# Inner feed-forward blocks: the two parts of x side by side in one 512-column product

## The chip, the cores and the metric

The kernel runs on one core of a Trainium2 chip. The metric is the device time of one execution in microseconds; 989.68 is the median of three runs (989.38 to 989.70). One further execution was profiled; the rows below come from it.

## The reference, cut to what matters

A transformer layer on 512 tokens of width 1024, all in float32: a feed-forward, a mixer (two kinds of attention), a second feed-forward, and a last normalization.

```python
def rmsnorm(x, g):
    y = x * lax.rsqrt(jnp.mean(x * x, axis=-1, keepdims=True) + NORM_EPS)
    return y * g

def swiglu(x, w_in, w_out):
    gate, up = jnp.split(x @ w_in, 2, axis=-1)     # w_in: 1024 x 5632
    return (jax.nn.silu(gate) * up) @ w_out        # w_out: 2816 x 1024

h = h + 0.5 * swiglu(rmsnorm(h, ffn1_norm), ffn1_w_in, ffn1_w_out)
h = h + hybrid_mixer(rmsnorm(h, mix_norm), ...)
h = h + 0.5 * swiglu(rmsnorm(h, ffn2_norm), ffn2_w_in, ffn2_w_out)
return rmsnorm(h, final_norm)
```

The change touches the products `x @ w_in` of both feed-forwards and what follows them up to `silu(gate) * up`.

## The kernel before, in words

**Parts.** A float32 operand is kept as two `float32r` tiles: the high part is a cast by ScalarE (`A.copy`), the low part is the rest, by a VectorE subtraction. A product of two such operands takes three matmuls: high weights by high x, high weights by low x, low weights by high x (lines 217 to 219 with 512 columns of x, lines 352 to 354 with 256). Tokens are the columns of x and of every result; features are the 128 partitions. The scale of the normalization, one number per token, is multiplied in later: `bc` holds it for all partitions.

**Feed-forward.** `ffn` treats the 2816 hidden features as FB = 22 blocks of 128. The first three blocks (`plain`) are computed directly with `mm3_steps`. The other 19 are the inner blocks. For each of them the 2x2 product (gate and up by first and second half of the tokens, with the sum over the 1024 features in two halves) is written with seven products of half the size instead of eight (the Winograd form of Strassen's method). `sums_of_x` makes the sums of x that this needs (`S` 1 to 4) once for a feed-forward, in high and low parts, a few instructions at a time beside the plain blocks. `sums_of_w` makes the sums of a block's weights (T1 to T4) and the parts of all seven weight pieces, one block ahead.

**One inner block.** `piece_of(j, p)` does product p of block j. `product` is four k steps of three matmuls each, 256 columns. Four results are built up in three places: `b1` (a bank of tag "sc"), one of two standing banks `b2` (tag "mm"), and `b3` (tag "mm"). Between products ScalarE or VectorE reads a bank and writes another: p = 1 copies b1 to b2 (line 575), p = 5 copies b3 to the tile su (582), p = 6 writes b2 + su into b3 (585), p = 7 makes the second half of `up` (594) and scales both (595, 596), p = 2 and p = 4 scale the two halves of `gate` by bc (588, 599) and take Silu (589, 600). `finish` multiplies the two (606) and `put_g` splits the result in parts (372, 374). On the two standing banks one opening matmul is issued (line 565) so that later products can add to what an engine wrote there.

**Order.** The hand-written order of products is, per block, p = 1, then p = 4 of the block before, then 5, 6, 2, 3, 7 (lines 609 to 612). After each product come one step of `finish`, one step of `side` (sums_of_w of the next block) and a share of the out-projection (`out_advance`), whose steps are 512-column triples of `mm3_steps`, each group of eight ending in an update of h on VectorE (427) and needing a split piece of w_out (404 on ScalarE, 405 on VectorE). Out-projection work comes in groups when the hidden blocks in ENDS are done, so some blocks have more of it between their products than others. From the program in this order the build lays out a fixed order for every engine, by its own estimates of durations and by program order as the priority; on the chip each engine takes its instructions in that order and waits where an operand is not ready.

**Buffers.** PSUM has tags "mm" (4 banks), "sc" (3) and "pv" (1). `tmp` tiles (10) serve su, z, gg and the raw pieces of w_out. SP issues all loads.

Of the kernel before, what the change touches and what calls it, by code (L numbers as in the profile page):

```python
# [12 lines left out]
AF = mybir.ActivationFunctionType  # L13
ALU = mybir.AluOpType
AX = mybir.AxisListType

P = 128
# [27 lines left out]
def tile_hybrid(ctx, tc, xT, f1_wi, f1_wo, wm_t, wm_n, cw1, cw2, small, wm_oa, wm_ob, wm_oc, f2_wi, f2_wo, const, out):  # L45
    nc = tc.nc
    V, A, PE = nc.vector, nc.scalar, nc.tensor
# [4 lines left out]
    def f(ap):  # L52
        return ap.bitcast(F32)

    def ps(tag="mm"):
        return psp.tile([P, 512], F32, tag=tag, name=tag, bufs=NB[tag])
# [4 lines left out]
    def ps_any():  # L61
        turn[0] += 1
        return ps(wide_ps[turn[0] % 5])

    def flat(dt=F32R):
        return sb.tile([P, 1024], dt, tag="u", name="u", bufs=NU)

    def unit(dt=F32R):
        return flat(dt).rearrange("p (a t) -> p a t", a=2)
# [4 lines left out]
    def tmp():  # L74
        return sb.tile([P, 512], F32, tag="tmp", name="tmp", bufs=NTMP)
# [156 lines left out]
    def sums_of_x(xs, gcol, XF):  # L232

        t1, t2 = slice(0, 256), slice(256, 512)
        xg = [None] * 4

        def scaled(*us):
            for u in us:
                t = xg[u] = unit(F32)
                for a in range(2):  # L240
                    k = 2 * u + a
                    gc = sm[:, gcol + k : gcol + k + 1]
                    if gcol == S_G2 and u % 2 == 0:
                        V.tensor_scalar(t[:, a, :], h[:, k, :], gc, None, op0=ALU.mult)
                    else:
                        A.activation(t[:, a, :], h[:, k, :], AF.Copy, scale=gc)

        def sums(kp, n):
            a, b = xg[kp], xg[2 + kp]
            s = flat(F32).rearrange("p (s k t) -> p s k t", s=2, k=2)  # L250
            if n == 0:
                V.tensor_tensor(s[:, 0], a[:, :, t2], b[:, :, t2], op=ALU.add)
                V.tensor_tensor(s[:, 1], s[:, 0], a[:, :, t1], op=ALU.subtract)
                s2[kp] = s[:, 1]
            else:
                V.tensor_tensor(s[:, 0], a[:, :, t1], a[:, :, t2], op=ALU.subtract)
                V.tensor_tensor(s[:, 1], b[:, :, t1], s2[kp], op=ALU.subtract)
            return s

        def high(s):  # L260
            sh = flat().rearrange("p (s k t) -> p s k t", s=2, k=2)
            A.copy(sh, s)
            return sh

        def low(s, sh, n):
            sl = flat().rearrange("p (s k t) -> p s k t", s=2, k=2)
            V.tensor_tensor(sl, s, f(sh), op=ALU.subtract)
            for m in range(2):
                XF["S", 2 * n + m + 1].extend((sh[:, m, k], sl[:, m, k]) for k in range(2))


        s2 = [None] * 2
        scaled(0)
        yield
        scaled(2)
        yield
        sa = sums(0, 0)
        yield
        scaled(1)
        sb_ = sums(0, 1)  # L280
        ha = high(sa)
        yield
        scaled(3)
        low(sa, ha, 0)
        yield
        hb = high(sb_)
        sc = sums(1, 0)
        yield
        low(sb_, hb, 1)
        sd = sums(1, 1)  # L290
        hc = high(sc)
        yield
        low(sc, hc, 0)
        hd = high(sd)
        yield
        low(sd, hd, 1)
        yield
        for name, ks, t in (("A11", 0, t1), ("A12", 4, t1), ("A22", 4, t2)):
            XF[name].extend((xs[k][:, 0, t], xs[k][:, 1, t]) for k in range(ks, ks + 4))

    def load_raw(wi, j):
        t = double()
# [43 lines left out]

    def product(o, w, x, first):

        for k in range(4):
            c = slice(k * P, (k + 1) * P)  # L350
            new = first and k == 0
            PE.matmul(o, w[0][:, c], x[k][0], start=new, stop=False, skip_group_check=not first)  # L352
            PE.matmul(o, w[0][:, c], x[k][1], start=False, stop=False, skip_group_check=not first)  # L353
            PE.matmul(o, w[1][:, c], x[k][0], start=False, stop=k == 3, skip_group_check=not first)  # L354

    def ffn(xs, acc, wi, wo, plain, gnext):

# [2 lines left out]
        bc = rcol = None  # L360
        gs, held = {}, []
        XF = {n: [] for n in ("A11", "A12", "A22", ("S", 1), ("S", 2), ("S", 3), ("S", 4))}
# [6 lines left out]
        def put_g(j, gg):  # L369
            u = unit()  # L370
            gs[j] = u
            A.copy(u[:, 0, :], gg)
            yield
            V.tensor_tensor(u[:, 1, :], gg, f(u[:, 0, :]), op=ALU.subtract)
            yield
# [130 lines left out]

        rc_at, bc_at = ((2, 6), (3, 4)) if early else ((0, 3), (1, 1))
        side.append(sums_of_x(xs, gcol, XF))
        done = []

# [13 lines left out]
        for n in range(2 * plain):  # L524
# [16 lines left out]
            else:  # L541
                wh, wl = next_w(2)
                o = ps_any()
# [16 lines left out]

        t1, t2 = slice(0, 256), slice(256, 512)

        banks = [ps()[:, t1] for _ in range(2)]
        for o in banks:
            PE.matmul(o, xs[0][:, 0, :P], xs[0][:, 0, t1], start=True, stop=True)

        live = {}
        later = []

        def piece_of(j, p):  # L570
            if p == 1:
                live[j] = ps("sc")[:, t1], banks[j % 2], None, None, None
                b1, b2 = live[j][:2]
                product(b1, WF.pop((j, "B11")), XF["A11"], True)
                A.copy(b2, b1)
                return
            b1, b2, b3, su, z = live[j]
            if p == 5:
                b3, su, z = ps()[:, t1], tmp(), tmp()
                live[j] = b1, b2, b3, su, z  # L580
                product(b3, WF.pop((j, "T1")), XF["S", 1], True)
                A.copy(su[:, t1], b3)
            elif p == 6:
                product(b2, WF.pop((j, "T2")), XF["S", 2], False)
                V.tensor_tensor(b3, b2, su[:, t1], op=ALU.add)
            elif p == 2:
                product(b1, WF.pop((j, "B21")), XF["A12"], False)
                V.tensor_tensor(z[:, t1], b1, bc[:, t1], op=ALU.mult)
                A.activation(z[:, t1], z[:, t1], AF.Silu)
            elif p == 3:  # L590
                product(b3, WF.pop((j, "B22")), XF["S", 4], False)
            elif p == 7:
                product(b2, WF.pop((j, "T3")), XF["S", 3], False)
                V.tensor_tensor(su[:, t2], b2, su[:, t1], op=ALU.add)
                V.tensor_tensor(su[:, t1], b3, bc[:, t1], op=ALU.mult)
                V.tensor_tensor(su[:, t2], su[:, t2], bc[:, t2], op=ALU.mult)
            elif p == 4:
                product(b2, WF.pop((j, "T4")), XF["A22"], False)
                V.tensor_tensor(z[:, t2], b2, bc[:, t2], op=ALU.mult)
                A.activation(z[:, t2], z[:, t2], AF.Silu)  # L600
                del live[j]
                later.append(finish(j, su, z))

        def finish(j, su, z):
            gg = tmp()
            V.tensor_tensor(gg, su, z, op=ALU.mult)
            yield from put_g(j, gg)

        order = []
        for j in range(plain, FB):  # L610
# [3 lines left out]
        for n, (j, p) in enumerate(order):  # L614
            if p == 1 and j + 1 < FB:
                side.append(sums_of_w(raws, wi, j + 1, WF))
            piece_of(j, p)
            while later and next(later[0], later) is later:
                later.pop(0)
            side_step()  # L620
            if p == 6 and j in ENDS:
                outs.append(out_steps(ENDS.index(j)))
            out_advance(0.7 if j >= ENDS[-2] else 0.6 if j < ENDS[1] else 1.0)
            if j >= FB - 1 and not side and len(opiece) < 4:
                out_split()
# [38 lines left out]
    xs = []  # L664
    first = []
# [33 lines left out]
    A.activation(late, f(xs[KB - 1][:, 0, 0:1]), AF.Copy, scale=0.0)  # L699
    state["squares"] = [(k, acc, late) for k in range(KB)]  # L700
    xs, acc = ffn(xs, acc, f1_wi, f1_wo, NP1, S_GM)


# [550 lines left out]
    for g in (1, 0):  # L1254
        for i in range(4):
            s = Swa(g, i)
            s.name, s.needs, s.share = ("s", g, i), [] if g else ["q10"], SHARE_S
            stages.append(s)
    for g in range(2):
        for i in range(4):  # L1260
            for b in (1, 2) if i else (0,):
                s = Nsa(g, i, b)
# [6 lines left out]


    ffn(nxs, nacc, f2_wi, f2_wo, NP2, None)


# [90 lines left out]
```

## Time and profile before

| | us |
|---|---|
| runs, median (lowest to highest) | 989.68 (989.38 to 989.70) |
| the profiled execution | 989.41 |
| its span | 987.5 |
| TensorE matmul busy | 972.7 (98%), 6228 matmuls |
| VectorE busy | 799.8 (81%) |
| ScalarE busy | 507.2 (51%) |
| DMA queue, all loads and stores | 92.59 MB, 27.1% of 16 engines' span |

The span is from the first to the last instruction; the execution's time is 1.9 us longer. A busy share is an average over stages: the inner blocks run from 43 to 335 us and from 661 to 950 us of the span, the mixer lies between. Matmuls overlap, so a matmul's listed duration is longer than the distance to the next one's start. VectorE and ScalarE instructions with no wait between them overlap by less than a tenth of a microsecond. The granted clock of TensorE is 1.00 (2.4 GHz) in all stretches used here.

### The profile page before, as it was taken

Reading aid. Unit: us, or ns where it says so; the run is one execution under the profiler, and the core shown is the slowest. Engines: PE = TensorE matmul, PEld = TensorE weight load, DVE = VectorE, ACT = ScalarE, POOL = GpSimd, SP = SyncE. Lnnn points to the kernel's source line nnn. Section 1 sums busy time; section 2 is a strip of 40 time slices with the busy share of each in tenths; the row PEclk is TensorE's granted clock in tenths of the full one; section 3 lists DMA queues with packets and bytes.
Section 4 is the critical chain, followed back from the end, with each engine's and each line's share of the span. In section 5 each row is a group of like instructions: output and inputs, shape, how many; then the busy total and the mean of one; then the engine's idle time right before and its main releaser. Section 6 shows DMA issues by size and latency. Waiting matters only on the chain.

```text
span 987.5 us, 15987 instructions
## 1 busy us (share of the span) xinstructions
PE 972.7 (98%) x6228; PEld 870.4 (88%) x6228; DVE 799.8 (81%) x1459; ACT 507.2 (51%) x1037; POOL 3.8 (0%) x7
## 2 busy tenths in 40 slices
PE   9999999999999999999999999999999999999997
PEld 7889999999999889888777878889999999999996
DVE  6999788787796575788799989999978878789664
ACT  8655344353444355554678776745434435344354
POOL 0000000000000000000000000000000000000000
PEclk9999999999999999999999999999999999999999
DMA  8142413233124313123310212224231322412112
GB/s 313 44 154 102 150 44 139 76 107 131 62 86 144 125 43 106 43 71 107 130 43 8 79 44 75 86 70 162 82 136 52 130 84 99 149 44 97 45 42 86
DMA packets 36075, 93.61 MB, mean 95 GB/s; under 512 B 4384, under 2 KB 8864, under 8 KB 36000
## 3 DMA queue, kind: packets, MB, share of 16 engines
q1 hardware_dynamic: 36000, 92.59, 27.1%
q8 instruction: 49, 0.80, 0.3%
q14 instruction: 26, 0.21, 0.1%
HBM read 88.87 MB, written 2.10 MB: 92 GB/s over the span
## 4 chain that ended last, share of the span: by engine, by line
PE 91%; DVE 5%; ACT 2%; issue 1%; DMA 1%; POOL 0%; SPq 0%; DVEq 0%; ACTq 0%
PE mm L353 9%; PE mm L352 9%; PE mm L354 9%; PE sc L217 8%; PE sc L219 8%; PE sc L218 8%; PE mm L217 4%; PE mm L219 4%; PE mm L218 4%; PE sc L353 3%; PE sc L354 3%; PE sc L352 3%; PE mm L936 2%; PE pv L973 2%; PE pv L974 2%; PE mm L792 1%
## 5 line engine op out<-in xcount | busy, mean ns | idle before, releaser
L354 PE MATMUL mm<-u 128*128 128x256 f32 x760 | 214.7, 283 | 0.0
L352 PE MATMUL mm<-u 128*128 128x256 f32 x760 | 214.4, 282 | 0.3 <-ACT u L328 0.3
L353 PE MATMUL mm<-u 128*128 128x256 f32 x760 | 214.6, 282 | 0.0
L352 PEld LDWEIGHTS mm<-u 128*128 128x128 f32 x760 | 144.5, 190 | 7.7 <-ACT u L328 0.5
L353 PEld LDWEIGHTS mm<-u 128*128 128x128 f32 x760 | 144.8, 191 | 5.5
L217 PE MATMUL sc<-u 128*128 128x512 f32 x364 | 144.3, 396 | 2.3 <-ACT u L404 2.1
L354 PEld LDWEIGHTS mm<-u 128*128 128x128 f32 x760 | 144.8, 191 | 0.5
L218 PE MATMUL sc<-u 128*128 128x512 f32 x364 | 143.6, 395 | 0.0
L219 PE MATMUL sc<-u 128*128 128x512 f32 x364 | 142.7, 393 | 0.0
L217 PE MATMUL mm<-u 128*128 128x512 f32 x220 | 89.8, 408 | 0.0
L219 PE MATMUL mm<-u 128*128 128x512 f32 x220 | 86.9, 395 | 0.0
L218 PE MATMUL mm<-u 128*128 128x512 f32 x220 | 86.5, 393 | 0.0
L354 PE MATMUL sc<-u 128*128 128x256 f32 x304 | 86.0, 283 | 0.3 <-DVE u L325 0.3
L353 PE MATMUL sc<-u 128*128 128x256 f32 x304 | 85.9, 283 | 0.0
L352 PE MATMUL sc<-u 128*128 128x256 f32 x304 | 85.7, 282 | 0.0
L219 PEld LDWEIGHTS sc<-u 128*128 128x128 f32 x364 | 68.4, 188 | 17.6 <-DVE u L405 1.8
L217 PEld LDWEIGHTS sc<-u 128*128 128x128 f32 x364 | 69.2, 190 | 9.7 <-ACT u L404 2.5
L404 ACT CAST u<-tmp 128x512 fp32r<-128x512 f32 (+1 forms) x96 | 55.0, 583 | 44.2 <-PE sc L219 21.0
L218 PEld LDWEIGHTS sc<-u 128*128 128x128 f32 x364 | 69.2, 190 | 6.3
L427 DVE SCALAR_TENSOR_TENSOR h<-sc,h 128x512 f32<-128x512 f32 x85 | 58.3, 686 | 11.7 <-PE sc L219 11.6
L405 DVE TENSOR_TENSOR u<-tmp,u 128x512 fp32r<-128x512 f32 (+1 forms) x96 | 60.8, 640 | 8.2 <-ACT u L404 8.0
L352 PEld LDWEIGHTS sc<-u 128*128 128x128 f32 x304 | 57.9, 190 | 2.6
(255 smaller groups left out, 2033.7 us busy)
## 6 DMA issues: line engine op xcount, KB each, us to landing
t<-in_f_wi_dram SPq DMA_DIRECT2D x88, 512.0 KB, 4.5
tmp<-in_f_wo_dram SPq DMA_DIRECT2D x80, 256.0 KB, 4.8
t<-in_wm_t_dram SPq DMA_DIRECT2D x13, 512.0 KB, 3.8
t<-in_cw_dram SPq DMA_DIRECT2D x8, 512.0 KB, 4.5
h<-in_xT_dram SPq DMA_DIRECT2D x4, 512.0 KB, 7.4
tmp<-in_f_wo_dram SPq DMA_DIRECT2D x16, 128.0 KB, 4.6
t<-in_wm_oa_dram SPq DMA_DIRECT2D x4, 512.0 KB, 4.1
out_dram<-tmp SPq DMA_DIRECT2D x8, 256.0 KB, 2.4
```

The lines of the kernel that those rows point to most:

```text
L217: PE.matmul(o, wh[:, c], xs[k][:, 0, :], start=s0, stop=False)
L218: PE.matmul(o, wh[:, c], xs[k][:, 1, :], start=False, stop=False)
L219: PE.matmul(o, wl[:, c], xs[k][:, 0, :], start=False, stop=s1)
L352: PE.matmul(o, w[0][:, c], x[k][0], start=new, stop=False, skip_group_check=not first)
L353: PE.matmul(o, w[0][:, c], x[k][1], start=False, stop=False, skip_group_check=not first)
L354: PE.matmul(o, w[1][:, c], x[k][0], start=False, stop=k == 3, skip_group_check=not first)
L404: A.copy(u[:, 0, :n], raw[:, :n])
L405: V.tensor_tensor(u[:, 1, :n], raw[:, :n], f(u[:, 0, :n]), op=ALU.subtract)
L427: V.scalar_tensor_tensor(h[:, i, :], o, 0.5, h[:, i, :], op0=ALU.mult, op1=ALU.add)
L936: PE.transpose(pt[:rows, r * P : (r + 1) * P], pl[r][:, cols], ident)
L973: PE.matmul(pv, v, u[:, 0, :], start=a, stop=False)
L974: PE.matmul(pv, v, u[:, 1, :], start=False, stop=b)
```

## The change

In the inner blocks the high and the low part of each piece of x lie side by side in one tile. One 512-column matmul multiplies both by the high weights; a 256-column matmul adds the low weights by the high part to the first half. So every result is 512 wide, and its halves have to be added before it is used: `joined` copies one half out of the bank on ScalarE and adds the other on VectorE. Scaling by bc and Silu are done on both token halves at once. The order of the products, the out-projection, the weights' sums and the plain blocks stay.

```diff
         def high(s):
-            sh = flat().rearrange("p (s k t) -> p s k t", s=2, k=2)
-            A.copy(sh, s)
-            return sh
-
-        def low(s, sh, n):
-            sl = flat().rearrange("p (s k t) -> p s k t", s=2, k=2)
-            V.tensor_tensor(sl, s, f(sh), op=ALU.subtract)
-            for m in range(2):
-                XF["S", 2 * n + m + 1].extend((sh[:, m, k], sl[:, m, k]) for k in range(2))
+            us = [flat().rearrange("p (a k t) -> p a k t", a=2, k=2) for _ in range(2)]
+            for m, u in enumerate(us):
+                A.copy(u[:, 0], s[:, m])
+            return us
+
+        def low(s, us, n):
+            for m, u in enumerate(us):
+                V.tensor_tensor(u[:, 1], s[:, m], f(u[:, 0]), op=ALU.subtract)
+                XF["S", 2 * n + m + 1].extend(u[:, :, k] for k in range(2))
...
-            XF[name].extend((xs[k][:, 0, t], xs[k][:, 1, t]) for k in range(ks, ks + 4))
+            XF[name].extend(xs[k][:, :, t] for k in range(ks, ks + 4))
...
-            PE.matmul(o, w[0][:, c], x[k][0], start=new, stop=False, skip_group_check=not first)
-            PE.matmul(o, w[0][:, c], x[k][1], start=False, stop=False, skip_group_check=not first)
-            PE.matmul(o, w[1][:, c], x[k][0], start=False, stop=k == 3, skip_group_check=not first)
+            PE.matmul(o, w[0][:, c], x[k], start=new, stop=False, skip_group_check=not first)
+            PE.matmul(o[:, :256], w[1][:, c], x[k][:, 0], start=False, stop=k == 3, skip_group_check=not first)
...
-        banks = [ps()[:, t1] for _ in range(2)]
+        banks = [ps() for _ in range(2)]
         for o in banks:
-            PE.matmul(o, xs[0][:, 0, :P], xs[0][:, 0, t1], start=True, stop=True)
+            PE.matmul(o, xs[0][:, 0, :P], xs[0][:, 0, :], start=True, stop=True)
...
+        def joined(z, o):
+
+            A.copy(z, o[:, t2])
+            V.tensor_tensor(z, o[:, t1], z, op=ALU.add)
+
         def piece_of(j, p):
             if p == 1:
-                live[j] = ps("sc")[:, t1], banks[j % 2], None, None, None
+                live[j] = ps("sc"), banks[j % 2], None, None, None
...
             if p == 5:
-                b3, su, z = ps()[:, t1], tmp(), tmp()
+                b3, su, z = ps(), tmp(), tmp()
                 live[j] = b1, b2, b3, su, z
                 product(b3, WF.pop((j, "T1")), XF["S", 1], True)
-                A.copy(su[:, t1], b3)
+                A.copy(su, b3)
             elif p == 6:
                 product(b2, WF.pop((j, "T2")), XF["S", 2], False)
-                V.tensor_tensor(b3, b2, su[:, t1], op=ALU.add)
+                V.tensor_tensor(b3, b2, su, op=ALU.add)
             elif p == 2:
                 product(b1, WF.pop((j, "B21")), XF["A12"], False)
-                V.tensor_tensor(z[:, t1], b1, bc[:, t1], op=ALU.mult)
-                A.activation(z[:, t1], z[:, t1], AF.Silu)
+                joined(z[:, t1], b1)
...
             elif p == 7:
                 product(b2, WF.pop((j, "T3")), XF["S", 3], False)
-                V.tensor_tensor(su[:, t2], b2, su[:, t1], op=ALU.add)
-                V.tensor_tensor(su[:, t1], b3, bc[:, t1], op=ALU.mult)
-                V.tensor_tensor(su[:, t2], su[:, t2], bc[:, t2], op=ALU.mult)
+                V.tensor_tensor(su, b2, su, op=ALU.add)
+                w = tmp()
+                joined(w[:, t1], b3)
+                V.tensor_tensor(w[:, t2], su[:, t1], su[:, t2], op=ALU.add)
+                V.tensor_tensor(w, w, bc, op=ALU.mult)
+                live[j] = b1, b2, b3, w, z
             elif p == 4:
                 product(b2, WF.pop((j, "T4")), XF["A22"], False)
-                V.tensor_tensor(z[:, t2], b2, bc[:, t2], op=ALU.mult)
-                A.activation(z[:, t2], z[:, t2], AF.Silu)
+                joined(z[:, t2], b2)
+                V.tensor_tensor(z, z, bc, op=ALU.mult)
+                A.activation(z, z, AF.Silu)
...
         def finish(j, su, z):
-            gg = tmp()
-            V.tensor_tensor(gg, su, z, op=ALU.mult)
-            yield from put_g(j, gg)
+            V.tensor_tensor(su, su, z, op=ALU.mult)
+            yield from put_g(j, su)
```

## Rows read from the trace of the kernel before

**Rows 1.** Page, part 1 (busy time) and part 4 (chain that ended last).

```profile
PE 972.7 (98%) x6228; PEld 870.4 (88%) x6228; DVE 799.8 (81%) x1459; ACT 507.2 (51%) x1037; POOL 3.8 (0%) x7
...
PE 91%; DVE 5%; ACT 2%; issue 1%; DMA 1%; POOL 0%; SPq 0%; DVEq 0%; ACTq 0%
```

**Rows 2.** Groups by line and shape: count, busy us, mean ns, idle before.

```profile
L352 PE MATMUL mm<-u 128*128 128x256 f32 x760 | 214.4, 282 | 0.3 <-ACT u L328 0.3
...
L352 PE MATMUL sc<-u 128*128 128x256 f32 x304 | 85.7, 282 | 0.0
...
L792 PE MATMUL mm<-u,t 128*128 128x62 f32 x128 | 16.9, 294 | 0.0
```

**Rows 3.** Timeline of PE, two stretches: start us, duration us, instruction.

```profile
144.61 0.28 PE L352 MATMUL sc<-u 128*128 128x256 f32 x1
...
146.05 0.28 PE L352 MATMUL mm<-u 128*128 128x256 f32 x1
...
187.19 0.40 PE L217 MATMUL sc<-u 128*128 128x512 f32 x1
...
188.58 0.28 PE L352 MATMUL mm<-u 128*128 128x256 f32 x1
```

**Rows 4.** Stretches: length, busy us of PE, PEld, DVE, ACT, POOL; clock; DMA.

```profile
22.00:46.40 24.40, 23.78 (x119) 19.78 (x118) 23.09 (x31) 16.79 (x24) 1.57 (x1) 1.00 0.13 47
46.40:102.80 56.40, 54.72 (x392) 51.56 (x392) 53.93 (x86) 26.25 (x48) 0.00 (x0) 1.00 0.37 132
662.70:717.80 55.10, 54.72 (x392) 51.54 (x391) 52.20 (x85) 26.14 (x49) 0.00 (x0) 1.00 0.39 135
150.60:213.20 62.60, 62.60 (x434) 58.16 (x433) 50.24 (x77) 26.80 (x44) 0.00 (x0) 1.00 0.28 101
200.30:213.20 12.90, 12.90 (x99) 12.32 (x98) 10.40 (x16) 6.60 (x11) 0.00 (x0) 1.00 0.20 69
```

**Rows 5.** Groups by line and shape, on DVE and ACT.

```profile
L585 DVE TENSOR_TENSOR mm<-mm,tmp 128x256 f32<-128x256 f32 x38 | 16.3, 428 | 0.7
...
L606 DVE TENSOR_TENSOR tmp<-tmp 128x512 f32<-128x512 f32 x38 | 26.2, 689 | 10.6 <-ACT tmp L600 10.6
...
L267 DVE TENSOR_TENSOR u<-u 128x1024 fp32r<-128x1024 f32 x8 | 9.8, 1221 | 0.1
...
L575 ACT COPY mm<-sc 128x256 f32<-128x256 f32 x38 | 13.6, 357 | 87.5 <-PE sc L354 87.5
...
L600 ACT ACTIVATE tmp<-tmp 128x256 f32<-128x256 f32 x38 | 15.9, 418 | 85.1 <-DVE tmp L599 85.1
...
L381 ACT ACTIVATE tmp<-tmp 128x512 f32<-128x512 f32 x6 | 3.8, 629 | 1.6 <-DVE tmp L379 1.6
```

**Rows 6.** Timeline of DVE: three instructions in a row.

```profile
180.66 0.68 DVE L405 TENSOR_TENSOR u<-tmp,u 128x512 fp32r<-128x512 f32 x1
...
181.26 0.42 DVE L595 TENSOR_TENSOR tmp<-mm,bc 128x256 f32<-128x256 f32 x1
...
181.59 0.42 DVE L596 TENSOR_TENSOR tmp<-tmp,bc 128x256 f32<-128x256 f32 x1
```

**Rows 7.** Timeline: adds of p = 6 and 7, and next user of the bank.

```profile
145.24 0.43 DVE L585 TENSOR_TENSOR mm<-mm,tmp 128x256 f32<-128x256 f32 x1
...
697.32 0.43 DVE L585 TENSOR_TENSOR mm<-mm,tmp 128x256 f32<-128x256 f32 x1
...
698.36 0.28 PE L352 MATMUL mm<-u 128*128 128x256 f32 x1
...
947.63 0.42 DVE L594 TENSOR_TENSOR tmp<-mm,tmp 128x256 f32<-128x256 f32 x1 [3.83 <-PE mm L354]
...
948.13 0.37 PE L352 MATMUL mm<-u 128*128 128x256 f32 x1
```

**Rows 8.** Timeline behind the last inner block.

```profile
952.52 0.69 DVE L374 TENSOR_TENSOR u<-tmp,u 128x512 fp32r<-128x512 f32 x1 [0.69 <-ACT u L372]
...
955.16 0.28 PE L451 MATMUL mm<-u 128*128 128x256 f32 x1
```

## The prediction, on record before the result

> **What bounds the kernel now.** I read the page first. TensorE is busy for 98% of the span, and the chain of waits that ended last runs on it for 91% and on VectorE for only 5% [rows 1]. So at first sight the tensor engine's own pace sets the time. Then I read the groups of instructions by line with shapes kept apart: the inner blocks issue 760 + 304 = 1064 matmuls on line 352 and as many on each of lines 353 and 354, all 128x256 [rows 2]. Their listed 282 ns overlap, so the price of one comes from starts in the timeline. The product that starts at 144.61 us has 12 of them before the next at 146.05: 120 ns each. Six 128x512 matmuls between 187.19 and 188.58 take 1.39 us: 232 ns each [rows 3]. Last I read the stretches: in the first four inner blocks of either feed-forward VectorE is busy for 53.93 of 56.40 us and 52.20 of 55.10 us, while in four blocks further on it is busy for 50.24 of 62.60 us [rows 4]. TensorE leads in the middle; at the start of each feed-forward VectorE has nearly nothing left, and at the first of these starts TensorE does wait (54.72 busy of 56.40). This split between stretches decides the change.
>
> **TensorE, removed.** Per k step, three 256-column matmuls (3 x 120 = 360 ns) become one of 512 and one of 256 (232 + 120 = 352 ns). The columns are the same; one matmul and one weight load go. 8 ns x 1064 = 8.5 us less. No row shows a 512 and a 256 with different weights alternating, so I bound it: 232 comes from six spacings whose single ones the timeline rounds between 0.23 and 0.24; at 235 the gain is 5.3 us, at 228 it is 12.8 us. I take 232, the mean.
>
> Of the operand's shape: x now enters as two runs of 256 columns, some 512 elements apart. No row shows that layout. The nearest is line 792, whose moving operand takes every eighth element: its 62 columns last 294 ns by the list, a dense 256 lasts 282 or 283 [rows 2]. So an uneven read costs between nothing and 11 ns, at most 11.7 us over 1064; a gain is excluded, the columns being the same. I take nothing, since a run of 256 is far nearer to dense than a step of eight, and keep the other end for rival D.
>
> The Trainium skill ("TensorE: Matmul & The Clock Gate", section "Back-to-back issue gap") gives the isolated spacing as 262 cycles for 256 columns and 518 for 512. At 2.4 GHz an estimate from it is 109 and 216 ns, thus 3 x 109 against 216 + 109: 2.5 ns a step, 2.7 us in all, and the sum below would end 5.8 us later. The measured 120 and 232 stand above both, so this trace does not bear that rule out, and the rows decide.
>
> Four opening matmuls on the two standing banks (two per feed-forward) go from 256 to 512 columns: 4 x 112 ns = +0.45 us on the path.
>
> **VectorE, added.** Everything that leaves a bank is now 512 wide until its halves are joined. Per block, by durations [rows 5]: the add into b3 (line 585) grows from 428 to about 690 ns, +0.26; the add into su at p = 7 likewise, +0.26; the three joined adds replace three 256-wide multiplications at the same 0.42; the add of su's halves replaces the multiplication of su's second half; two 512-wide multiplications by bc are new, 0.69 each. Sum +1.90 us a block. Behind one another VectorE's instructions start sooner than they last: a 512-wide one at 180.66, the next at 181.26, the next after a 256-wide at 181.59, so 0.60 and 0.33 [rows 6]. By these it is 2 x 0.27 + 2 x 0.60 = +1.74 us. In full queues I use 1.74, as upper end 1.90. Over 38 blocks that is 66 to 72 us of VectorE.
>
> **ScalarE, added.** Two copies out of a bank double in width and three copies of 256 are new (0.36 each), while two Silu of 256 become one of 512. A copy of 512 I estimate at 0.57, from 0.357 for 256 and the 0.21 between a Silu of 512 and one of 256 [rows 5]. That is +1.3 us a block, 5.2 in four blocks where it is busy 26.80 of 62.60 [rows 4]: covered. What it adds in waits is that each joined add on VectorE stands behind a ScalarE copy of the same bank; queued behind that add are the weight splits, the out-projection splits and the updates of h, and TensorE waits for those only about a block later.
>
> **sums_of_x.** One VectorE subtraction of 1024 (1221 ns) becomes two of 512, and one ScalarE cast becomes two. Two of 0.69 against 1.22 [rows 5] is +0.16, eight times. They lie in a stretch where VectorE is busy 23.09 of 24.40 us before the first inner block [rows 4], so about half comes through: 0.6 us for both feed-forwards, bounds 0 and 1.3.
>
> **First four blocks of each feed-forward.** TensorE needs 4 x 28 x 8 ns = 0.9 us less. VectorE has 2.47 and 2.90 us idle and gets 4 x 1.74 = 6.96 us more. What does not fit is 6.96 + 0.9 - 2.47 = 5.4 and 6.96 + 0.9 - 2.90 = 5.0 us. VectorE may come out of the stretch late by what TensorE tolerates: in the second feed-forward's third block the add into b3 starts at 697.32, lasts 0.43, and TensorE's product that needs it starts at 698.36 [rows 7], so 0.6 us is in reserve there; in blocks with more out-projection work between there is more. I let 1.5 us be carried over each time: stalls of 3.9 + 3.5 = 7.4 us. Ends: 0, if splits made a block ahead can give way, and 11.7 with 1.90 and nothing carried.
>
> **The steady four-block cycle.** 62.60 - 50.24 = 12.4 us idle [rows 4], against 7.0 to 7.6 us more work and 0.9 us less time: 3.9 to 4.5 us are left, so VectorE fits on the mean. It doesn't in the block in which no out-projection is left: there it has 10.40 busy of 12.90 [rows 4], leaving 2.5 against 1.74 + 0.2; and the add into b3 starts 145.24, ends 145.67, with TensorE's use at 146.05 [rows 3, 7]. The reserve of 0.38 loses 0.26 by the longer add, and before that add now stand a 512-wide multiplication and a longer Silu. I charge 0.4 us (between 0 and 1.0), for six such blocks: 2.4 us. In the last block of each feed-forward the add at p = 7 starts 947.63, lasts 0.42, and TensorE overwrites its bank from 948.13 [rows 7]: 0.08 in reserve against 0.26 more, 0.2 us twice: 0.4.
>
> The chain behind the very last product is longer by a copy and a multiplication, some 1.2 us. Its low part is made at 952.52 + 0.69 = 953.21, and the fourth product of the closing stage, the first that wants it, starts at 955.16 [rows 8]: hidden.
>
> No DMA, buffer count or queue of SP is moved; tmp tiles stay three per block.
>
> **Sum**, against the profiled execution's 989.41 us (span 987.5 and 1.9 around it, 0.27 below the median 989.68): 989.41 - 8.5 + 0.45 + 7.4 + 0.6 + 2.4 + 0.4 = 991.8. With the 0.27 to the median about 992.
>
> **Rivals.**
> (B) VectorE's extra work is absorbed. For it: it already ran 53.93 of 56.40 us with one real stall, and the weights' splits are made a block ahead, so late ones hurt nobody. Against it: the instruction order on each engine is fixed at build time and what is late comes late in that order, the urgent adds too. Then the 7.4 and 2.4 shrink to about 2: 989.7 - 8.5 + 0.45 + 0.6 + 0.4 + 2 = 984.6.
> (C) VectorE becomes the bound in the steady cycle too, the other side. Place: the joined adds. Each holds VectorE's queue for a ScalarE copy, 0.36 and about 0.05 of signalling; three per block make 4.9 us a cycle. Together with 0.69 us that line 374 waits for ScalarE today [rows 8], 2.8 a cycle, the need is 50.24 + 7.6 + 4.9 + 2.8 = 65.5 against 61.7. It decides as soon as more than 4.5 us of the cycle's waits stay unfilled. All unfilled: 3.8 us in each of some seven cycles, 27 us; half of that is nearer, since in the crowded first blocks nearly no wait stays unfilled: 992 + 13 = 1005.
> (D) The gain of pace does not come: a 512 read as two runs costs 240 ns, within the 11 ns above. Against it stands only how even the spacings of [rows 3] are. It takes the 8.5 us back: 1000.5.
>
> **How the numbers follow.** Forecast 45%, own range 988 to 997; B 27%; C 15%; D 10%; 3% for others. A measurement of this kernel can tell about 0.2% (2 us) from no change. Faster than 987.7: nearly all of B and a little of the forecast, 0.28. Between 987.7 and 991.7: a third of the forecast, 0.17. Slower: 0.55. The range 981 to 1005 takes in B with the larger gain of pace (12.8) and half of C.
>
> **What would show it.** In the changed profile: 1064 fewer matmuls and weight loads; starts 0.23 after a 512 and 0.12 after a 256 in the inner blocks (if not, D). VectorE's busy time 66 to 73 us higher, ScalarE's about 50. Waits of TensorE's inner products for VectorE's adds or splits within about 57 us of either start and in blocks without out-projection (if none, B). In the steady cycle 61.7 us for four blocks with VectorE near 94% is the forecast; 63 us or more is C. I am wrong altogether if TensorE waits nowhere more than now, or if a cycle grows by over 2 us.

## The result, and the profile after

The changed kernel takes 981.61 us (median of four runs, 981.38 to 981.78), against 989.58 for the kernel before, run beside it on the same chip: the ratio is 0.992, with an interval from 0.9902 to 0.9937. It is faster by 8.0 us. The forecast was 992.0 us, slower by 2.4; rival B, at 984.6, had the right side. The profiled span is 980.0 us against 987.5, at a granted clock of 0.998 of 2.4 GHz.

The page of the changed kernel, parts 1 and 4, against [rows 1]:

```profile
PE 963.8 (98%) x5164; PEld 813.0 (83%) x5164; DVE 857.5 (88%) x1543; ACT 553.2 (56%) x1121; POOL 3.7 (0%) x7
...
PE 93%; DVE 3%; ACT 2%; DMA 1%; issue 0%; POOL 0%; SPq 0%; DVEq 0%; ACTq 0%
```

There are 1064 matmuls fewer. VectorE is busy 57.7 us more, ScalarE 46.0 us more, and VectorE's share of the chain that ended last fell from 5 to 3%. So VectorE did get the work that the prediction feared, and the path runs through it less than before.

The changed kernel's groups by line, the answer to [rows 2] (count, busy us, mean ns, idle before):

```profile
L353 PE MATMUL mm<-u 128*128 128x512 f32 x760 | 275.0, 396 | 0.5 <-DVE mm L590 0.5
L354 PE MATMUL mm<-u 128*128 128x256 f32 x760 | 212.5, 280 | 0.1
L217 PE MATMUL sc<-u 128*128 128x512 f32 x364 | 144.2, 396 | 3.5 <-ACT u L372 2.6 <-ACT u L404 0.5 <-ACT u L105 0.3
```

Line 353 reads x as two runs of 256, line 217 reads a dense 512: both are listed with 396 ns. A listed duration is longer than the distance to the next start, so the starts decide: behind line 353 the next matmul starts 233 ns later, behind line 217 it does so after 232 (medians). The uneven read costs nothing that these rows show.

Its timeline of TensorE, the answer to [rows 3] (start us, duration us, instruction):

```profile
151.42 0.40 PE L353 MATMUL mm<-u 128*128 128x512 f32 x1
151.66 0.28 PE L354 MATMUL mm<-u 128*128 128x256 f32 x1
151.77 0.40 PE L353 MATMUL mm<-u 128*128 128x512 f32 x1
...
154.24 0.40 PE L217 MATMUL sc<-u 128*128 128x512 f32 x1
...
155.64 0.40 PE L353 MATMUL sc<-u 128*128 128x512 f32 x1
```

From 151.42 to 151.77 a step takes 0.35 us. Over the whole trace the median distances in the inner products are 233 ns behind a 512 and 117 ns behind the 256 that follows it, 350 ns a step, against 3 x 120 = 360 before. The means of the distances that hold no wait are 349.8 ns a step now and 358.1 before, a gain of 8.3. The six 512s between the last two lines still take 0.23 us each.

The stretches of [rows 4] in the changed kernel: the first four inner blocks of the first feed-forward, four steady blocks, the last of these alone (the one without out-projection between its products), and the first four of the second feed-forward (bounds, length, busy us of PE, PEld, DVE, ACT, POOL; clock; DMA):

```profile
45.60:103.50 57.90, 55.54 (x288) 46.10 (x288) 56.38 (x89) 31.62 (x57) 0.00 (x0) 1.00 0.35 117
150.30:211.70 61.40, 61.40 (x322) 52.17 (x321) 56.22 (x86) 31.61 (x52) 0.00 (x0) 1.00 0.29 103
199.10:211.70 12.60, 12.60 (x70) 10.81 (x69) 11.55 (x20) 7.80 (x13) 0.00 (x0) 1.00 0.17 50
658.90:714.60 55.70, 54.38 (x288) 46.02 (x287) 54.77 (x88) 30.54 (x55) 0.00 (x0) 1.00 0.38 128
```

The steady cycle went from 62.60 to 61.40 us, and TensorE is busy all the time: by starts, 1.0 of the 1.2 us are its 112 inner steps, 9 ns each, and 0.2 the out-projection triples among them. VectorE is busy 92% of it. At the two starts VectorE is busy 97 and 98%, and there TensorE does wait.

The changed kernel's groups on VectorE and ScalarE, the answer to [rows 5]:

```profile
L590 DVE TENSOR_TENSOR mm<-mm,tmp 128x512 f32<-128x512 f32 x38 | 26.4, 695 | 2.0 <-PE mm L354 1.7
L573 DVE TENSOR_TENSOR tmp<-mm,tmp 128x256 f32<-128x256 f32 x76 | 32.0, 421 | 11.9 <-ACT tmp L572 11.5
L602 DVE TENSOR_TENSOR tmp<-tmp,bc 128x512 f32<-128x512 f32 x38 | 26.1, 687 | 0.1
...
L572 ACT COPY tmp<-mm 128x256 f32<-128x256 f32 x76 | 28.2, 371 | 64.7 <-PE mm L354 64.1
L580 ACT COPY mm<-sc 128x512 f32<-128x512 f32 x38 | 21.7, 570 | 68.2 <-PE sc L354 68.2
```

The single durations came as forecast (0.69, 0.42, 0.69; the copy of 512 at 0.57). A joined add stands idle for its ScalarE copy 11.5 / 76 = 0.15 us on the mean, not the 0.41 of rival C.

**Account.** I summed the distances from each matmul's start to the next one's over both traces. The inner products went from 385.5 to 375.0 us (-10.45), the 512-column triples of lines 217 to 219 from 413.6 to 416.0 (+2.4; their growth is in the out-projection of the first blocks), and the rest, opening matmuls included, grew by about 0.5. Together that is the 7.5 us of the span.

The 10.45 are not pace alone, since a distance also holds the wait that follows its matmul. Behind inner products the kernel before has 4.5 us of waits, the changed kernel 2.8. Without them the inner products take 381.0 and 372.2 us: the gain of pace is 8.8 us.

The +2.4 are waits. The groups of 0.5 us and more among TensorE's waits within the inner stages (line, releaser: us in total, times, longest):

```profile
PE sc L217 <- ACT u L372: 2.6, 2, 1.3
...
PE mm L353 <- DVE mm L590: 0.5, 1, 0.5
...
PE sc L217 <- ACT u L404: 0.5, 1, 0.5
```

By the distances between starts, four of the changed kernel's waits are over 0.6 us, all in the first four blocks of a feed-forward: 0.67 at 66.8, 0.63 at 69.5, 1.48 at 94.2 and 1.48 at 705.4 us. The kernel before had one such wait, 1.84 us at 50.2, behind an inner product. All waits within the first four blocks, short ones included, add up to 6.0 us, against 3.8 before.

### The profile page after: what moved, and what is told of

It reads as the page before. It is cut to its first block, busy times and chain, and to the rows that moved or that the text cites. A ratio compares the mean times of both kernels' runs of the same rounds, so it can differ in the third digit from the quotient of the medians.

```text
span 980.0 us, 14002 instructions
## 1 busy us (share of the span) xinstructions
PE 963.8 (98%) x5164; PEld 813.0 (83%) x5164; DVE 857.5 (88%) x1543; ACT 553.2 (56%) x1121; POOL 3.7 (0%) x7
## 4 chain that ended last, share of the span: by engine, by line
PE 93%; DVE 3%; ACT 2%; DMA 1%; issue 0%; POOL 0%; SPq 0%; DVEq 0%; ACTq 0%
PE mm L353 18%; PE mm L354 9%; PE sc L217 8%; PE sc L219 8%; PE sc L218 8%; PE sc L353 7%; PE mm L217 5%; PE mm L219 5%; PE mm L218 5%; PE sc L354 3%; PE mm L943 2%; PE pv L980 2%; PE pv L981 2%; PE mm L799 1%; PE sc L934 1%; PE sc L935 1%
## 5 line engine op out<-in xcount | busy, mean ns | idle before, releaser
L353 PE MATMUL mm<-u 128*128 128x512 f32 x760 | 275.0, 396 | 0.5 <-DVE mm L590 0.5
L354 PE MATMUL mm<-u 128*128 128x256 f32 x760 | 212.5, 280 | 0.1
L353 PEld LDWEIGHTS mm<-u 128*128 128x128 f32 x760 | 142.6, 188 | 35.1 <-DVE mm L590 0.8
L354 PEld LDWEIGHTS mm<-u 128*128 128x128 f32 x760 | 143.2, 188 | 6.3 <-DVE u L331 0.4
L217 PE MATMUL sc<-u 128*128 128x512 f32 x364 | 144.2, 396 | 3.5 <-ACT u L372 2.6
L219 PE MATMUL sc<-u 128*128 128x512 f32 x364 | 143.0, 394 | 0.0
L218 PE MATMUL sc<-u 128*128 128x512 f32 x364 | 142.9, 393 | 0.0
L353 PE MATMUL sc<-u 128*128 128x512 f32 x304 | 110.5, 396 | 0.0
L217 PE MATMUL mm<-u 128*128 128x512 f32 x220 | 89.8, 408 | 0.0
L219 PE MATMUL mm<-u 128*128 128x512 f32 x220 | 86.9, 395 | 0.0
L218 PE MATMUL mm<-u 128*128 128x512 f32 x220 | 86.5, 393 | 0.0
L354 PE MATMUL sc<-u 128*128 128x256 f32 x304 | 85.1, 280 | 0.2 <-DVE u L325 0.2
L217 PEld LDWEIGHTS sc<-u 128*128 128x128 f32 x364 | 68.3, 188 | 19.6 <-ACT u L372 3.5
L219 PEld LDWEIGHTS sc<-u 128*128 128x128 f32 x364 | 68.3, 188 | 17.1 <-DVE u L405 1.7
L218 PEld LDWEIGHTS sc<-u 128*128 128x128 f32 x364 | 68.4, 188 | 7.4
L353 PEld LDWEIGHTS sc<-u 128*128 128x128 f32 x304 | 57.1, 188 | 13.3
L572 ACT COPY tmp<-mm 128x256 f32<-128x256 f32 x76 | 28.2, 371 | 64.7 <-PE mm L354 64.1
L354 PEld LDWEIGHTS sc<-u 128*128 128x128 f32 x304 | 57.3, 188 | 3.5 <-DVE u L325 0.6
L580 ACT COPY mm<-sc 128x512 f32<-128x512 f32 x38 | 21.7, 570 | 68.2 <-PE sc L354 68.2
```

The lines of the kernel that those rows point to most:

```text
L217: PE.matmul(o, wh[:, c], xs[k][:, 0, :], start=s0, stop=False)
L218: PE.matmul(o, wh[:, c], xs[k][:, 1, :], start=False, stop=False)
L219: PE.matmul(o, wl[:, c], xs[k][:, 0, :], start=False, stop=s1)
L353: PE.matmul(o, w[0][:, c], x[k], start=new, stop=False, skip_group_check=not first)
L354: PE.matmul(o[:, :256], w[1][:, c], x[k][:, 0], start=False, stop=k == 3, skip_group_check=not first)
L572: A.copy(z, o[:, t2])
```

## The experiments

Four theories meet here. **W**: VectorE's busy time in the crowded blocks contains weight splits made long before they are needed; the work of the exits lets them give way. **P**: the added work costs about what I charged, and a larger gain of pace covers it. After run 5 two more: **U**: what waits are left come from urgent instructions standing in the order behind work done early, so they go when that work starts later. **C** (not rival C of the prediction): VectorE's capacity at the starts sets the time. Every run was timed in three rounds, beside the kernel before (medians 989.4 to 989.6).

**1. The exits without the merged product.** The 512 is taken apart; the second half still goes to the second half of the bank.

```diff
-PE.matmul(o, w[0][:, c], x[k], start=new, ...)
-PE.matmul(o[:, :256], w[1][:, c], x[k][:, 0], ...)
+PE.matmul(o[:, :256], w[0][:, c], x[k][:, 0], start=new, ...)
+PE.matmul(o[:, 256:], w[0][:, c], x[k][:, 1], start=False, ...)
+PE.matmul(o[:, :256], w[1][:, c], x[k][:, 0], ...)
```

> The changed kernel with the merged matmul taken apart again: three matmuls of 256 columns a step, the low part of x written to the second half of the bank; everything behind the products stays as in the changed kernel. It carries VectorE's and ScalarE's added work without the gain of pace. Theory W (the added work is carried, since what gives way are the splits of weights, made long before their use): 981.6 + 10.4 = 992, that is 2 to 3 us above the kernel before. Theory P (the prediction: what does not fit in the first blocks comes out as stalls, 7 to 11 us): 997 to 1001.

Measured: 989.50 us, ratio 1.0001 (0.9991 to 1.0011). On its page VectorE has the changed kernel's load:

```profile
PE 973.2 (99%) x6228; PEld 870.8 (88%) x6228; DVE 857.5 (87%) x1543; ACT 554.4 (56%) x1121; POOL 3.2 (0%) x7
```

So 57.7 us more on VectorE cost nothing on the whole at the old pace of TensorE. That is against P, and 2.5 us below W too. It does not mean that no wait came. New ones stand where the changed kernel has them:

```profile
PE sc L217 <- ACT u L373: 1.4, 2, 0.7
```

But the waits of the kernel before (1.84 and 0.54 us at the two starts) are gone, and within the first four blocks the sum stays the same, 3.6 us against 3.8. The build's new order moves waits both ways, so a difference of some two microseconds between two kernels need not come from the work that was added.

**2. The merged product without the exits.** Only the first half of each bank is read, in the way of the kernel before; the product of the high weights by x's low part is left out of the result.

```diff
-A.copy(su, b3)
+A.copy(su[:, t1], b3[:, t1])
-V.tensor_tensor(b3, b2, su, op=ALU.add)
+V.tensor_tensor(b3[:, t1], b2[:, t1], su[:, t1], op=ALU.add)
...
```

> The changed kernel's merged products with the exits of the kernel before: only the first half of each bank is read, so the product of the low part of x is left out of the result. It has the gain of pace without the added work. Both theories: 989.6 - 10.4 + 0.2 = 979.4. W: at most 2.4 us below the changed kernel. P with a gain larger than 8.5 us that hid the stalls: 971 to 974, that is 8 us or more below the changed kernel.

Measured: 975.87 us, ratio 0.9859 (0.9844 to 0.9874), lower than the 979.4 that both expected. It is 5.7 us below the changed kernel, where W had allowed 2.4 and P wanted 8. Inner products take 373.4 us and triples 412.1: beside the pace, waits of the kernel before are gone too (within the first four blocks 1.1 us are left). So at the new pace the exits do have a price, 981.61 - 975.87 = 5.7 us.

**3. Extra work for VectorE, in both kernels.** Idle 512-wide additions in every block, three in the kernel before and two in the changed one.

```diff
+dump = sb.tile([P, 512], F32, tag="dump", name="dump", bufs=1)
...                                    # at p = 3 of each block
+for _ in range(3):                    # 2 in the changed kernel
+    V.tensor_tensor(dump, bc, bc, op=ALU.add)
```

> The kernel before with three more 512-wide VectorE additions in each inner block, at p = 3, whose results nobody reads: 1.8 to 2.07 us a block, the size of what the change adds. Theory W: 989.6 + 1 to 4 us. Theory P: 989.6 + 8 to 11 us.

> The changed kernel with two more 512-wide VectorE additions in each inner block, 1.2 to 1.4 us, whose results nobody reads. The steady four blocks have 5.1 us of VectorE idle left in 61.4, so 4.8 to 5.5 us more just fills them. Theory W: the crowded first four blocks lose what they get, 2 x 4 x 1.3 = 10 us at most, the steady ones 0 to 1 us each: 986 to 996. If time beyond the listed idle were still to be had: below 984.

Measured: 991.52 us in the kernel before, ratio 1.0021 (1.0011 to 1.0030): 61 us more of VectorE cost 2.0. In the changed kernel 989.96, ratio 1.0004 (0.9995 to 1.0014): 41 us more cost 8.4. Both are within what W expected. The second shows that little room is left after the change, in its order.

**4. The exits' adds kept behind the splits.** The adds of lines 590, 598 and 573 may not pass a weight subtraction that stands ahead of them in the program.

```diff
+def behind(ins):
+    tc.add_manual_dep(ins.ins, last_split[0].ins.name, ..., reason="order")
...
-V.tensor_tensor(b3, b2, su, op=ALU.add)
+behind(V.tensor_tensor(b3, b2, su, op=ALU.add))
```

> The changed kernel with one rule more for VectorE's order: the adds that read a bank (into b3, into su, and the joined ones) stay behind the weight subtractions that the program issues ahead of them. Theory W: the adds then wait for splits that nobody needs yet; at least 0.5 us in each block, 10 to 25 us slower than the changed kernel, with waits of the inner products for the add into b3. Rival N (VectorE simply has enough idle time, its order does not matter): within 2 us of the changed kernel.

Measured: 1006.67 us, ratio 1.0169 (1.0154 to 1.0185), 25 us slower than the changed kernel. Its waits of TensorE (the edit shifts lines by nine: 340 is a weight subtraction, 381 the cast of g):

```profile
PE mm L363 <- DVE u L340: 8.2, 16, 0.8
PE sc L217 <- ACT u L381: 6.2, 8, 0.9
PE mm L362 <- ACT u L337: 2.0, 1, 2.0
PE sc L218 <- DVE u L383: 1.8, 8, 0.2
```

The same instructions in another order cost 25 us, in every cycle. The waits don't fall on the adds themselves, as I had thought, but on what comes late behind them: the split of the next weights and the cast of g.

**5. The splits begun later.** The weights' sums of the next block start at the fourth product of the order (p = 6) instead of the first (p = 1).

```diff
-if p == 1 and j + 1 < FB:
+if p == 6 and j + 1 < FB:
     side.append(sums_of_w(raws, wi, j + 1, WF))
```

> The changed kernel with the sums of a block's weights begun three products later (at p = 6 of the block before instead of p = 1). Theory W: the time between a weight split and its first use is what carries VectorE's added work; with some 6 us of it gone at least 5 us slower than the changed kernel. Rival N (idle time as such is enough): within 2 us of it.

Measured: 976.68 us, ratio 0.9871 (0.9856 to 0.9885). W had expected at least 5 us slower, since it held that the early start is what gives room; it is 4.9 us faster. That part of W fell, and U took its place. The lead of a split, the time from its end to the first matmul that reads it, is smaller here, but 0.3 us or more is left behind the first block. The stretch of the first four blocks, in this kernel:

```profile
45.60:103.50 57.90, 57.79 (x304) 49.05 (x305) 56.51 (x88) 31.82 (x56) 0.00 (x0) 1.00 0.33 112
```

VectorE is busy 56.51 us here and 56.38 in the changed kernel, the same 97%. Yet TensorE is busy 57.79 instead of 55.54, and all waits within the first four blocks of both feed-forwards fell from 6.0 to 1.3 us. Busy share doesn't tell whether TensorE has to wait; the order does.

**6. Other ways at the same waits.** The out-projection of a group begun at p = 2 instead of p = 6; and the first two inner blocks of each feed-forward in the form of the kernel before.

```diff
-if p == 6 and j in ENDS:
+if p == 2 and j in ENDS:
```

```diff
-piece_of(j, p)
+(piece_n if j < plain + 2 else piece_of)(j, p)      # piece_n: as before, 256 wide
```

> The changed kernel with each group of the out-projection begun one product later (behind p = 2 instead of p = 6). Theory W: of the waits left, the two of 1.5 us are the first out-projection step waiting for the last block's g, whose chain became longer by the joining; they go, 978.6. If they only move: 981 to 982.

> The changed kernel with the first two inner blocks of either feed-forward done as before the change (three matmuls of 256, 256-wide exits), the other 17 as changed. Theory W: the four blocks give back 4 x 28 x 10 ns = 1.1 us of pace and save 4 x 1.74 us of VectorE where it has none left; the waits of 0.67 and 0.63 us go and the two of 1.48 shrink: 978 to 980.5. If the waits come from ScalarE or from the order alone: 982.5.

Measured: 981.85 us, ratio 0.9922 (0.9907 to 0.9937), no gain; the two waits of 1.48 only moved, to 93.7 and 705.3 us. The mixed version took 977.44, ratio 0.9879 (0.9862 to 0.9895), a little below what W expected: the four waits are gone, with one of 0.45 us left at 109.8. So the price sits in the first blocks, and it is not set by when the out-projection is handed out.

**7. The later start, tested further.** In the kernel before (p = 6), and in the changed one later still (p = 3, the sixth product).

> The kernel before with the weights' sums begun at p = 6 instead of p = 1. Theory U (formed after the last runs: what stalls TensorE is an urgent instruction queued behind weight splits that are made earlier than they are needed; VectorE's capacity is not the limit): the waits of 1.84 and 0.54 us at the two starts go, 987 to 988.5. Theory W (the time between a split and its use is what is needed): 991 or more.

> The changed kernel with the weights' sums begun at p = 3, two products later again: the split of T1 is then issued two products ahead of its use. Theory U has a lower end, where the splits themselves become what TensorE waits for: 985 to 1000, with the inner products waiting for the lines 325 and 331. If there is reserve even then: 976 to 978.

Measured: 988.00 us, ratio 0.9985 (0.9976 to 0.9994), and 994.47, ratio 1.0054 (1.0037 to 1.0071), both within what U expected. In the first, though, only the wait of 0.54 us went; that of 1.84 shrank to 1.3, so the time agrees with U and the place only in part. The waits of the second:

```profile
PE mm L353 <- ACT u L339: 4.7, 8, 1.7
PE sc L354 <- DVE u L336: 2.2, 6, 0.4
PE sc L217 <- ACT u L372: 1.5, 6, 0.3
```

Now TensorE waits for the weights' casts and splits (339 and 336; I had named 325 and 331). Three products later is a gain of 4.9 us, five are a loss of 12.9.

**8. Capacity, once the order is better.** The splits from p = 6, with two idle additions a block; and the splits from p = 6, with the narrow exits of run 2 (which leaves out the same product).

> The changed kernel with the weights' sums begun at p = 6 and the two idle 512-wide additions of VectorE in each block. Theory U: 977 to 982, where the same two additions cost 8.4 us with the sums begun at p = 1. Theory C (VectorE's capacity is the limit, and 976.7 was only a better filling): 985 or more.

> Merged products, exits as before the change (the product of the low part of x is left out of the result), the weights' sums begun at p = 6. Theory U: what is left of the price of the exits is the distance to 976.7: 975 to 976, under 1.5 us. Theory C: 972 or less.

Measured: 984.51 us, ratio 0.9952 (0.9937 to 0.9967), and 974.48, ratio 0.9850 (0.9835 to 0.9865). Both lie between the theories. The exits cost 976.68 - 974.48 = 2.2 us in this order and 5.7 in the changed kernel's. Two further additions cost 7.8 us here and 8.4 there. So the later start takes away 3.5 of the 5.7 us, which is U's part. For the two further additions C, with 985 or more, came nearer; no other amount was tried in this order.

## Why the prediction was wrong, step by step

**What held.** The gain of pace was right in kind and size: 8.5 us forecast by 8 ns a step, 8.8 measured by 8.3. Both sides of it were 2 ns off, 349.8 where I had summed 232 + 120 = 352, and 358.1 where I had 360, and these errors cancel. The Trainium skill ("TensorE: Matmul & The Clock Gate", section "Back-to-back issue gap") gives 262 and 518 cycles, from which I had estimated 2.5 ns a step; this trace shows 8.3, and does not bear that out. Rival D is refuted by the starts, 233 ns behind line 353 and not 240. The tail stayed hidden: no wait stands on the closing stage's lines 451 to 453. Rival C did not come: 61.40 us a cycle, not 63 or more.

**The step that failed** is "First four blocks of each feed-forward", with its sentence "What does not fit is 6.96 + 0.9 - 2.47 = 5.4 and 6.96 + 0.9 - 2.90 = 5.0 us", of which 7.4 us were to come through as stalls. It took VectorE's 2.47 and 2.90 idle us for all the room there was. The waits over 0.6 us are 4.3 us in the changed kernel against 1.8 in the one before, so 2.4 us of new stalls came, and run 1 got all the exits' work in with no more waiting in these blocks than before. In the busy 53.93 of 56.40 us were weight splits that nobody waited for yet. In the kernel before, a block's splits (lines 325, 331, 336 and 341) ended 4.5 to 18 us ahead of the first matmul that read them, the first block of the first feed-forward excepted. The changed kernel took its added work out of that lead. At the fourth inner block of either feed-forward the lead of line 325 fell from 9.6 to 2.6 us and that of line 331 from 7.7 and 7.0 to 4.0; in the steady part that of line 331 fell from 6.7 to 13.9 us to 5.2 to 11.4. No inner product behind the first block waited for a split. That lead was the room, and the prediction had priced only the idle time. It had named this itself, as the lower end of the term ("0, if splits made a block ahead can give way") and as rival B with 27%, and put it aside.

**The reserve of the add** was the second error of that kind. I had let 1.5 us be carried over because the add into b3 has 0.6 us in reserve in its place, and charged 2.4 us for "the block in which no out-projection is left". By its own numbers VectorE's work did fit in that block, 2.5 us idle against 1.74 + 0.2, so only the reserve carried the charge. Both took the instruction's place in VectorE's order as given. But the build lays out a new order. Timeline of the changed kernel in that block, against the adds of [rows 7]:

```profile
206.07 0.69 DVE L590 TENSOR_TENSOR mm<-mm,tmp 128x512 f32<-128x512 f32 x1
206.67 1.22 DVE L331 TENSOR_TENSOR u<-t,u 128x1024 fp32r<-128x1024 f32 x1
...
207.21 0.40 PE L353 MATMUL mm<-u 128*128 128x512 f32 x1
```

The add into b3 now stands ahead of the weight subtraction of line 331 (in the kernel before that subtraction was at 206.77 and the add behind it, at 207.90). It ends at 206.76, 0.45 us before TensorE writes its bank: as much reserve as before the change, with 0.26 us more to do. In the whole steady part no wait came of it, so the 2.4 us were nought, and so were the 0.4 us of the last blocks: these terms and the 5.0 us too much at the starts make up 7.8 of the 10.0 us by which the sum of 991.8 lay above the profiled 981.8. The rest is spread over small terms. My argument against rival B, that "the urgent adds too" come late in a fixed order, is what the runs contradict: the order is fixed on the chip, but it is laid out anew for each program.

**Where the order does fail** shows the longest wait, in the changed kernel:

```profile
91.80 0.42 DVE L573 TENSOR_TENSOR tmp<-mm,tmp 128x256 f32<-128x256 f32 x1 [0.60 <-ACT tmp L572]
92.14 0.68 DVE L324 TENSOR_TENSOR t<-t,t 128x512 f32<-128x512 f32 x1
92.74 0.68 DVE L607 TENSOR_TENSOR tmp<-tmp,bc 128x512 f32<-128x512 f32 x1
93.34 0.68 DVE L325 TENSOR_TENSOR u<-t,u 128x512 fp32r<-128x512 f32 x1
93.46 0.63 ACT L608 ACTIVATE tmp<-tmp 128x512 f32<-128x512 f32 x1 [1.69 <-DVE tmp L607]
93.94 0.69 DVE L330 TENSOR_TENSOR t<-t,t 128x512 f32<-128x512 f32 x1
94.55 0.68 DVE L613 TENSOR_TENSOR tmp<-tmp 128x512 f32<-128x512 f32 x1
...
95.26 0.62 ACT L372 CAST u<-tmp 128x512 fp32r<-128x512 f32 x1 [0.88 <-DVE tmp L613]
...
95.93 0.50 PE L217 MATMUL sc<-u 128*128 128x512 f32 x1 [1.32 <-ACT u L372]
```

The out-projection needs g. Between the joined add of line 573 and the multiplication by bc that needs it (line 607) VectorE takes line 324, a subtraction for the next block's weights: 0.60 us. Silu ends at 94.09, but the multiplication of line 613 starts only at 94.55, behind line 330, another of these. The two places hold up g by about 1.0 of the 1.48 us; that the rest is the longer chain of the exits was not tested. The wait of 0.63 us at 69.5 has its place on ScalarE: there the cast of w_out's piece (line 404) stands at 69.88, behind two casts of the next block's weights (lines 328 and 334, from 67.98). The prediction had looked for stalls of the inner products; the costly ones fall on the out-projection.

**Smaller terms.** VectorE's busy time rose 57.7 us, 1.5 a block where I had 1.74; that fewer instructions now stand alone and more overlap would explain it, but no run tests it. The four opening matmuls and `sums_of_x` were charged 1.05 us together; about 0.5 is left for them and all else. By the steps as they came out, from the profiled execution before: 989.4 - 8.8 of pace - 1.7 of waits behind inner products + 2.4 in the triples + 0.5 = 981.8.

**Open.** How much of the waits is VectorE's order and how much ScalarE's was not separated. Every edit also gives the build another order of all engines, so in the runs that add or take away work the share of the work and that of the new order were not separated either. Runs 4 and 5 come closest to it: they have the changed kernel's instructions and differ from it in order alone. The later start and the old form of the first two blocks were not tried together. The best kernel run is that of run 5, 976.68 us, 4.9 below the changed kernel and 12.8 below the one before.

## What to carry to other kernels

A high busy share of an engine beside the bound one is not yet a lack of room: ask of each of its instructions how long its reader still waits, and count the lead of work done ahead as room along with the idle time. A reserve read at one instruction holds only while the order holds; where the build lays out the order, a change of load moves urgent and early work against each other, to either side. When such work is begun early, try its start some products later and stop where the bound engine begins to wait for it.

## What was not expected of the hardware

A 256-column matmul that follows a 512 with other weights takes 117 ns to the next start, not the 120 between 256s (medians). Reading the moving operand as two runs of 256 costs nothing that shows against a dense 512 (233 and 232 ns to the next start). VectorE can be busy without a gap and TensorE not wait: in the changed kernel from 74.00 to 86.59 us, in the third inner block, both are busy for 12.59 of 12.59 us.
